# The late modulation's rows loaded in quarters on GpSimd's own queue, into a buffer of their own, begun while RWKV is prepared

## The chip, the cores and the metric

The kernel runs on one core of a Trainium2 chip. The metric is the time of one execution on the device in microseconds (us): a median over runs, and beside it one execution taken by the hardware profiler, from which all rows below are read. In the profile PE is TensorE (PEld its weight loads), DVE is VectorE, ACT is ScalarE, POOL is GpSimd, SP is SyncE, which here only issues DMAs. "SPq" and "POOLq" are the queues in which an engine's DMAs wait in order.

## What is computed

The reference runs two transformer blocks, one after the other, over 512 tokens of width 1024 in float32. Only the first has the part that is changed: all its norms are modulated by a vector that comes from a condition `c`.

```python
mod = jax.nn.silu(c) @ ada_w[l] + ada_b[l]
sh_m, sc_m, g_m, sh_f, sc_f, g_f = jnp.split(mod[:, None, :], 6, axis=-1)

h = rmsnorm(x, norm_g[l, 0]) * (1.0 + sc_m) + sh_m
p = h @ w_in[l]
p_a, p_b, p_c = split_cols(p, (N_RWKV_IN, N_FOX_IN, N_NSA_IN))
y_a = rwkv7_mix(p_a, ...)
y_b = fox_mix(p_b, ...)
y_c = nsa_mix(p_c, ...)
y = jnp.concatenate([y_a, y_b, y_c], axis=-1) @ w_out[l]
x = x + g_m * rmsnorm(y, norm_g[l, 1])
h = rmsnorm(x, norm_g[l, 2]) * (1.0 + sc_f) + sh_f
f = conv_ffn(h, ...)
x = x + g_f * rmsnorm(f, norm_g[l, 3])
```

`sh_m` and `sc_m` are needed at the start. The other four sections of `mod`, here called the late modulation, are needed only after `w_out`. `ada_w` is 1024 x 6144, 24 MB, of which 16 MB are late. In `rwkv7_mix` the key is normalised head by head (`kk / max(norm(kk), 1e-12)`), and the head's output `y` is normalised by its mean and variance after the recurrence.

## The kernel before

**Stages.** From the start to about 60 us the first modulation and the RWKV projection run. Then come `prep(0)` and `prep(1)`, which make the operands of the RWKV recurrence for two halves of its channels, then `core(0)` and `core(1)` in turns, which run the recurrence in chunks of 64 tokens. Beside the cores run `side` (`compress`, `fox`, `stacks`: the compressed keys, the FoX attention, keys laid out for the NSA attention). All of these generators leave gaps on PE, and `fill(n)` puts matmuls of the projections (`proj_t`, `proj_n`) into them, one or two after each of their steps. After the cores come the NSA attention, `project_out` and the rest of the kernel.

**What sets the order.** A scheduler orders the instructions of each engine by the order in which the code emits them and by its own estimate of when each is ready. Each engine then runs its list strictly in order and waits where an operand or a free buffer is missing. A DMA belongs to the list of the engine that issues it. Nearly all loads are on SP's.

**Streamed weights.** `Weights.load` (L263) loads the next block of weights, 128 partitions x up to 1024, on SP's queue (L269) into the tile `raw`, which has three buffers. `Weights.next` then has ScalarE write the rounded high part `whi` (L278) and VectorE the rest `wlo` (L279), three buffers each. Projections use both.

**The late modulation.** `some_ada` (L623) treats one of 16 matrices (sections 1 and 2, eight row blocks `k`), 128 x 2048 each. It takes two `raw` buffers in turn, loads 512 KB into each on SP's queue (L631), and GpSimd multiplies each of the eight 128 x 256 pieces by a column of `sil` (L635 the first, L637 the others) and adds them up in `am` (L638), four buffers. A call later (`owing`) PE sums `am` over the partitions with `ones` and VectorE adds the bias into `mod`. `some_ada` is called on every second turn of the core loop (AE = 2, L956), and the rest after it (`some_ada(99)`).

**Head norms.** `head_rsq` (L721) runs in each `prep` (on `kk`) and at the end of each `core` (on `y`). PE sums squares by head (`psr<-x,sq`), VectorE writes `hv` (L298 is its helper's line), GpSimd raises it to -0.5 as `hr` (L733), VectorE spreads it as `nr` (L735), and PE transposes that back (L738). GpSimd also turns the loaded masks into 8 bit as `im` (L688). In `compress`, `kk` (L1020, L1021) and the weights `w` (L1029) come on SP's queue, VectorE adds a position term into `kr`, PE multiplies by `w` into `psa`, and VectorE and ScalarE form `ch` for a second matmul.

Of the kernel before, what the change touches and what calls it, by code (L numbers as in the profile page):

```python
# [10 lines left out]
F32 = mybir.dt.float32  # L11
# [7 lines left out]
P = 128  # L19
# [236 lines left out]
class Weights:  # L256


    def __init__(self, nc, pool, src, raw_bufs, bufs):
        self.nc, self.pool, self.src, self.raw_bufs, self.bufs = nc, pool, src, raw_bufs, bufs  # L260
        self.i = 0

    def load(self, label):  # L263
        nc, i = self.nc, self.i
        lab, bl = PLAN[i]
        assert lab == label, (lab, label)
        n = sum(len(c) for _, _, c in bl)
        raw = self.pool.tile([P, 1024], F32, name="raw", bufs=self.raw_bufs)
        nc.sync.dma_start(raw[:, :n], self.src[i][:, :n])  # L269
        self.i += 1  # L270
        return raw[:, :n]
# [12 lines left out]
def two_blocks(ctx, tc, ins, out):  # L284
    nc = tc.nc
    S, V, G, PE = nc.scalar, nc.vector, nc.gpsimd, nc.tensor
# [18 lines left out]
    MUL, ADD, SUB, MAX, MIN = ALU.mult, ALU.add, ALU.subtract, ALU.max, ALU.min  # L305

    const = ctx.enter_context(tc.tile_pool(name="const", bufs=1))
    wpool = ctx.enter_context(tc.tile_pool(name="wts", bufs=1))
    upool = ctx.enter_context(tc.tile_pool(name="u", bufs=1))
    dram = ctx.enter_context(tc.tile_pool(name="dram", bufs=1, space=bass.MemoryType.DRAM))  # L310
    W = Weights(nc, wpool, ins["wst"], 3, 3)
# [22 lines left out]
    sil = const.tile([P, 8], F32, name="sil")  # L334
# [283 lines left out]

    owing = []

    def some_ada(n=1):

        for _ in range(n):  # L623
            if not todo and not owing:
                return
            if todo:
                sec, k = todo.pop(0)
                am = st.tile([P, 256], F32, name="am", bufs=4)
                for q in range(2):
                    aw = wpool.tile([P, 4, 256], F32, name="raw", bufs=W.raw_bufs)  # L630
                    nc.sync.dma_start(aw.rearrange("p a b -> p (a b)"), ins["ada"][sec, k][:, q * 1024:(q + 1) * 1024])  # L631
                    for r in range(4):
                        s = sil[:, 4 * q + r:4 * q + r + 1]
                        if q + r == 0:
                            G.tensor_scalar(am, aw[:, r], s, 1.0, op0=MUL, op1=MUL)  # L635
                            continue
                        G.tensor_scalar(aw[:, r], aw[:, r], s, 1.0, op0=MUL, op1=MUL)  # L637
                        G.tensor_tensor(am, am, aw[:, r], op=ADD)  # L638
                owing.append((sec, k, am))
            if len(owing) > 1 or not todo:  # L640
                sec, k, am = owing.pop(0)
                ps = bank(f"r{k % 2}", 2)
                for s in range(2):
                    mm(ps[:, s:s + 1], am[:, s * P:(s + 1) * P], ones[:, 0:1])
                j = 16 * sec + k
                tt(mod[:, j:j + 9:8], ps[:, :2], vc("ada_b", j, 9)[:, ::8], ADD)
# [303 lines left out]
        return lambda ps: act(dst, ps, AF.Copy, scale=scale)  # L950

    LO = 0
    FP, FN, NS, FC, NA, OR, AE = 1.6,2.4,3,(2.2,2.6),5,0,2
    jobs = [proj_t("nsa", copy_to(kcv[0])), proj_t("nsa", copy_to(kcv[1])), proj_n("nsa_n", 280, 2, evac_n),
            proj_n("fox_n", 384, 2, lambda b, ps: act(fv[:, b], ps, AF.Copy))]
    for j in range(3):  # L956
# [15 lines left out]
    def fill(n):  # L972
        with later():
            owed[0] += n
            while owed[0] >= 1:
                owed[0] -= 1
                next(work[0], None)
# [182 lines left out]

    kst = []
    prep, core, spare = rwkv(phA.enter_context(tc.tile_pool(name="rp", bufs=1, reuse_waits="tile")))
    for t in range(2):
        for _ in prep(t):
            fill(FP)
    for _ in work[0]:
        pass
    pA.close()
# [22 lines left out]
    for _ in work[0]:  # L1191
        pass
    some_ada(99)
    phA.close()
    nm[0] = 2
    psm = blk.enter_context(tc.tile_pool(name="psb", bufs=1, space=PSUM, reuse_waits="tile"))
# [345 lines left out]
    q = SqSum(fp)  # L1542
# [538 lines left out]
```

## Time and profile before

| | us |
|---|---|
| median of 3 runs | 2184.73 |
| lowest and highest | 2183.6, 2187.89 |
| the profiled execution | 2183.81 |
| its span in the trace | 2182.0 |

The late modulation and the stages around it lie in the first sixth of the span. A row of a timeline gives the start, the duration, the engine, the line, the operation, what it writes and reads with their shapes, and in square brackets how long the engine had been idle before it and on what. A row of a window gives the busy time of each engine within it; PEclk is the TensorE clock that was granted, as a share of 2.4 GHz, so 0.50 is the level of 1.2 GHz.

### The profile page before, as it was taken

The page shows a single profiled execution, that of the slowest core. Times are in us where ns is not written, and L with a number is a line of the kernel's source. Part 1 is how long each engine was busy: PE and PEld are TensorE (multiplying, and loading weights), DVE is VectorE, ACT ScalarE, POOL GpSimd, SP SyncE. Part 2 cuts the span into 40 slices and gives each one's busy share as a digit, 9 for nine tenths or more (in the row PEclk, how much of TensorE's full clock was granted, in tenths as well). Part 3 has the DMA queues.
Part 4 walks back from the last instruction along what each step waited for, and adds up shares of the span by engine and source line. Part 5 has one row for each costly group of instructions (what it writes and reads, how often), then busy time and mean ns, then how long its engine had stood idle before and what let it go on. Part 6 is the DMA issues. An engine that isn't in the chain of part 4 may idle for free.

```text
span 2182.0 us, 31649 instructions
## 1 busy us (share of the span) xinstructions
PE 2134.6 (98%) x12498; PEld 1762.1 (81%) x12498; DVE 1142.8 (52%) x2171; ACT 785.9 (36%) x1332; POOL 496.4 (23%) x538
## 2 busy tenths in 40 slices
PE   7989999999999999899999999999999999999999
PEld 5878777667888888788888899998877888888887
DVE  6553445666752664653344449957554455433442
ACT  4422223553542442332222335445453233222221
POOL 3168662232000000320011024333221022100110
PEclk9989998998999999999999999999999999999999
DMA  8344335102532222222222343342352222222222
GB/s 309 102 145 157 109 137 145 40 21 88 165 133 97 98 97 87 70 96 98 97 98 98 126 152 107 100 128 76 111 145 86 95 92 96 97 97 97 98 97 85
DMA packets 84846, 238.31 MB, mean 109 GB/s; under 512 B 13970, under 2 KB 21448, under 8 KB 84570
## 3 DMA queue, kind: packets, MB, share of 16 engines
q1 hardware_dynamic: 78874, 226.19, 30.9%
q0 software_dynamic: 5104, 9.52, 1.2%
q8 instruction: 98, 1.61, 0.3%
q10 hardware_dynamic: 720, 0.57, 0.1%
q14 instruction: 50, 0.41, 0.1%
HBM read 216.02 MB, written 15.33 MB: 106 GB/s over the span
## 4 chain that ended last, share of the span: by engine, by line
PE 75%; DVE 1%; ACT 1%; issue 0%; POOL 0%; ACTq 0%; DVEq 0%; POOLq 0%
PE mm L288 68%; PE pS L288 3%; PE pO L288 2%; PE pT L1666 1%; PE pT L1649 1%; PE pT L288 0%; PE pst L288 0%; DVE xa L303 0%; PE psm L288 0%; DVE wlo L279 0%; DVE tmp L1487 0%; PE pso L288 0%; DVE ul L303 0%; PE lps L288 0%; ACT whi L278 0%
## 5 line engine op out<-in xcount | busy, mean ns | idle before, releaser
L278 ACT ACTIVATE whi<-raw 128x1024 fp32r<-128x1024 f32 (+4 forms) x312 | 325.7, 1046 | 836.0 <-PE mm L288 619.8
L279 DVE TENSOR_TENSOR wlo<-raw,whi 128x1024 fp32r<-128x1024 f32 (+4 forms) x303 | 373.9, 1235 | 343.3 <-ACT whi L278 339.6
L288 PE MATMUL mm<-ul,whi 128*128 128x512 f32 (+1 forms) x1280 | 494.9, 388 | 1.8 <-DVE ul L303 1.8
L288 PE MATMUL mm<-uh,wlo 128*128 128x512 f32 (+1 forms) x1280 | 494.4, 387 | 0.5 <-DVE wlo L279 0.5
L288 PE MATMUL mm<-uh,whi 128*128 128x512 f32 (+1 forms) x1280 | 489.7, 388 | 2.1 <-ACT uh L291 1.2
L288 PEld LDWEIGHTS mm<-ul,whi 128*128 128x128 f32 x1280 | 241.7, 189 | 52.5 <-DVE ul L303 2.8
L288 PEld LDWEIGHTS mm<-uh,whi 128*128 128x128 f32 x1280 | 239.9, 189 | 52.3 <-ACT uh L291 1.8
L288 PEld LDWEIGHTS mm<-uh,wlo 128*128 128x128 f32 x1280 | 241.8, 189 | 48.8 <-DVE wlo L279 0.9
L288 PE MATMUL mm<-hh,wlo 128*128 128x512 f32 (+1 forms) x550 | 209.3, 381 | 0.0
L288 PE MATMUL mm<-hl,whi 128*128 128x512 f32 (+1 forms) x550 | 209.3, 381 | 0.0
L288 PE MATMUL mm<-hh,whi 128*128 128x512 f32 (+1 forms) x550 | 208.4, 381 | 0.0
L1516 POOL TENSOR_TENSOR gg<-gg,R 128x512 f32<-128x512 f32 x44 | 77.4, 1762 | 473.4 <-ACT gg L291 473.4
L288 PE MATMUL mm<-whi,uh 128*128 128x256 f32 (+1 forms) x488 | 140.5, 288 | 0.0
L288 PE MATMUL mm<-whi,ul 128*128 128x256 f32 (+1 forms) x488 | 139.8, 287 | 0.0
L288 PE MATMUL mm<-wlo,uh 128*128 128x256 f32 (+1 forms) x488 | 139.2, 285 | 0.0
L288 PEld LDWEIGHTS mm<-hl,whi 128*128 128x128 f32 x550 | 103.4, 188 | 19.8
L288 PEld LDWEIGHTS mm<-hh,whi 128*128 128x128 f32 x550 | 103.4, 188 | 19.7
L288 PEld LDWEIGHTS mm<-hh,wlo 128*128 128x128 f32 x550 | 103.4, 188 | 19.6
L291 ACT ACTIVATE p<-p,smin 128x128 f32<-128x128 f32 (+4 forms) x136 | 81.8, 602 | 92.8 <-DVE smin L1077 52.6
L294 DVE TENSOR_TENSOR gh<-mm,gg 128x512 f32<-128x512 f32 x44 | 30.4, 691 | 131.1 <-PE mm L288 125.5
L288 PEld LDWEIGHTS mm<-whi,ul 128*128 128x128 f32 x488 | 93.1, 191 | 1.7 <-issue 1.5
L288 PEld LDWEIGHTS mm<-whi,uh 128*128 128x128 f32 x488 | 93.0, 191 | 1.4 <-issue 0.4
(532 smaller groups left out, 3433.8 us busy)
## 6 DMA issues: line engine op xcount, KB each, us to landing
raw<-in_wst_dram SPq DMA_DIRECT2D x294, 512.0 KB, 3.2
raw<-in_ada_dram SPq DMA_DIRECT2D x32, 512.0 KB, 4.7
aw<-in_ada_dram SPq DMA_DIRECT2D x16, 512.0 KB, 8.4
raw<-in_wst_dram SPq DMA_DIRECT2D x8, 448.0 KB, 6.0
ka<-d POOLq DMA_DIRECT2D x1, 3570.0 KB, 49.5
k<-d POOLq DMA_DIRECT2D x1, 2556.0 KB, 17.1
part<-in_x_dram SPq DMA_DIRECT2D x4, 512.0 KB
xa<-in_x_dram SPq DMA_DIRECT2D x8, 256.0 KB, 3.6
```

The costliest lines, as they stand in the source:

```text
L278: nc.scalar.activation(hi[:, :n], w, AF.Copy)
L279: (e or nc.vector).tensor_tensor(lo[:, :n], w, hi[:, :n].bitcast(F32), op=ALU.subtract)
L288: PE.matmul(o, l, r, start=start, stop=stop)
L291: S.activation(o, i, f, **kw)
L294: V.tensor_tensor(o, a, b, op=op)
L1516: G.tensor_tensor(g, g, R, op=MUL)
L1649: PE.transpose(ps[:, (j * nb + b) * P:(j * nb + b + 1) * P], xn[:, (b * n + j) * P:(b * n + j + 1) * P], ident)
L1666: PE.transpose(ps[:, j:j + P], p[:, o + j:o + j + P], ident)
```

## The change

The late matrices no longer use `raw` and SP's queue. They come as 64 quarters of 256 KB, issued by GpSimd, into the two halves of one tile `raws`, and the load of the next quarter is issued ahead of the work on the present one. `raws` is taken from the streamed weights: `raw` keeps two buffers, and a weight goes to the third, now `raws`, only while `W.spare` is true, which it isn't from before `prep` until after `some_ada(99)`. `some_ada` is called on every tenth step of both `prep`, four times in all, and on every third turn of the core loop instead of every second.

```diff
--- before.py
+++ after.py
@@ -258,14 +258,17 @@
 
     def __init__(self, nc, pool, src, raw_bufs, bufs):
         self.nc, self.pool, self.src, self.raw_bufs, self.bufs = nc, pool, src, raw_bufs, bufs
-        self.i = 0
+        self.i = self.n = 0
+        self.spare = True
 
     def load(self, label):
         nc, i = self.nc, self.i
         lab, bl = PLAN[i]
         assert lab == label, (lab, label)
         n = sum(len(c) for _, _, c in bl)
-        raw = self.pool.tile([P, 1024], F32, name="raw", bufs=self.raw_bufs)
+        last = self.spare and self.n % self.raw_bufs == self.raw_bufs - 1
+        self.n += 1
+        raw = self.pool.tile([P, 1024], F32, name="raws" if last else "raw", bufs=1 if last else self.raw_bufs - 1)
         nc.sync.dma_start(raw[:, :n], self.src[i][:, :n])
         self.i += 1
         return raw[:, :n]
@@ -618,24 +621,44 @@
 
     owing = []
 
+    def pieces():
+
+        ax = wpool.tile([P, 4, 256], F32, name="raws", bufs=1)
+        order = [(sec, k, q) for sec in (1, 2) for k in range(8) for q in range(4)]
+
+        def load(i):
+            sec, k, q = order[i]
+            h = ax[:, 2 * (i % 2):2 * (i % 2) + 2]
+            G.dma_start(h.rearrange("p a b -> p (a b)"), ins["ada"][sec, k][:, q * 512:(q + 1) * 512])
+            return h
+
+        h = load(0)
+        for i in range(len(order)):
+            nxt = load(i + 1) if i + 1 < len(order) else None
+            yield h
+            h = nxt
+
+    rows = pieces()
+
     def some_ada(n=1):
 
         for _ in range(n):
             if not todo and not owing:
                 return
             if todo:
-                sec, k = todo.pop(0)
-                am = st.tile([P, 256], F32, name="am", bufs=4)
-                for q in range(2):
-                    aw = wpool.tile([P, 4, 256], F32, name="raw", bufs=W.raw_bufs)
-                    nc.sync.dma_start(aw.rearrange("p a b -> p (a b)"), ins["ada"][sec, k][:, q * 1024:(q + 1) * 1024])
-                    for r in range(4):
-                        s = sil[:, 4 * q + r:4 * q + r + 1]
+                am = None
+                for q in range(4):
+                    h = next(rows)
+                    if q == 0:
+                        sec, k = todo.pop(0)
+                        am = st.tile([P, 256], F32, name="am", bufs=4)
+                    for r in range(2):
+                        s = sil[:, 2 * q + r:2 * q + r + 1]
                         if q + r == 0:
-                            G.tensor_scalar(am, aw[:, r], s, 1.0, op0=MUL, op1=MUL)
+                            G.tensor_scalar(am, h[:, 0], s, 1.0, op0=MUL, op1=MUL)
                             continue
-                        G.tensor_scalar(aw[:, r], aw[:, r], s, 1.0, op0=MUL, op1=MUL)
-                        G.tensor_tensor(am, am, aw[:, r], op=ADD)
+                        G.tensor_scalar(h[:, r], h[:, r], s, 1.0, op0=MUL, op1=MUL)
+                        G.tensor_tensor(am, am, h[:, r], op=ADD)
                 owing.append((sec, k, am))
             if len(owing) > 1 or not todo:
                 sec, k, am = owing.pop(0)
@@ -950,7 +973,7 @@
         return lambda ps: act(dst, ps, AF.Copy, scale=scale)
 
     LO = 0
-    FP, FN, NS, FC, NA, OR, AE = 1.6,2.4,3,(2.2,2.6),5,0,2
+    FP, FN, NS, FC, NA, OR, AE = 1.6,2.4,3,(2.2,2.6),5,0,3
     jobs = [proj_t("nsa", copy_to(kcv[0])), proj_t("nsa", copy_to(kcv[1])), proj_n("nsa_n", 280, 2, evac_n),
             proj_n("fox_n", 384, 2, lambda b, ps: act(fv[:, b], ps, AF.Copy))]
     for j in range(3):
@@ -1160,9 +1183,12 @@
 
     kst = []
     prep, core, spare = rwkv(phA.enter_context(tc.tile_pool(name="rp", bufs=1, reuse_waits="tile")))
+    W.spare = False
     for t in range(2):
-        for _ in prep(t):
+        for i, _ in enumerate(prep(t)):
             fill(FP)
+            if i % 10 == 9:
+                some_ada()
     for _ in work[0]:
         pass
     pA.close()
@@ -1191,6 +1217,7 @@
     for _ in work[0]:
         pass
     some_ada(99)
+    W.spare = True
     phA.close()
     nm[0] = 2
     psm = blk.enter_context(tc.tile_pool(name="psb", bufs=1, space=PSUM, reuse_waits="tile"))
```

Lines of the changed kernel are shifted: L733 is L756 there, L635, L637 and L638 are L658, L660 and L661, L269 is L272, L278 is L281.

On GpSimd, before, from the end of the first modulation (`am` from `aw`) on. Both `hr` here are those of `prep`:

```order
L573 TENSOR_TENSOR am_562<-am_562,aw 128x256 x3
L577 TENSOR_TENSOR am<-am,am_562 128x256
L688 CAST im<-imf 128x320 x2
L733 TENSOR_TENSOR hr<-hv,mhalf 128x8 x2
L635 TENSOR_SCALAR am<-raw,sil 128x256
L637 TENSOR_SCALAR raw<-raw,sil 128x256 x3
L638 TENSOR_TENSOR am<-am,raw 128x256
L637 TENSOR_SCALAR raw<-raw,sil 128x256 x2
L638 TENSOR_TENSOR am<-am,raw 128x256
```

GpSimd, changed, the last rows ahead of the first `hr` (`am` and `raws` belong to the late matrices):

```order
L660 TENSOR_SCALAR raws<-raws,sil 128x256
L661 TENSOR_TENSOR am<-am,raws 128x256 x2
L658 TENSOR_SCALAR am<-raws,sil 128x256
L660 TENSOR_SCALAR raws<-raws,sil 128x256
L632 DMA raws<-in_ada_dram 128x512
L661 TENSOR_TENSOR am<-am,raws 128x256
L632 DMA raws<-in_ada_dram 128x512
L660 TENSOR_SCALAR raws<-raws,sil 128x256 x2
L661 TENSOR_TENSOR am<-am,raws 128x256
L756 TENSOR_TENSOR hr<-hv,mhalf 128x8
L660 TENSOR_SCALAR raws<-raws,sil 128x256 x2
```

Ahead of the first `hr` there are now 20 scalings (TENSOR_SCALAR), 16 additions (TENSOR_TENSOR on `raws`), the two casts and 9 loads, all behind the first modulation's last addition but for two further loads that stand before it. Between the first and the second `hr` stand 14 scalings, 13 additions and 7 loads. The cores' two `hr` were behind all late matrices before and are so now.

On SP's queue, before, from the last weights loaded during `prep` on:

```order
L269 DMA raw<-in_wst_dram 128x1024 x2
L631 DMA raw<-in_ada_dram 128x1024
L993 DMA cf<-in_cmat_dram 128x128
L631 DMA raw<-in_ada_dram 128x1024
L269 DMA raw<-in_wst_dram 128x1024
L631 DMA raw<-in_ada_dram 128x1024 x3
L1020 DMA kk_1255<-kcv_109 64x512
L1021 DMA kk_1255<-kcv_109 64x511
L1009 DMA dcum<-cum 6x512
L1020 DMA kk_1260<-kcv_109 64x512
L1021 DMA kk_1260<-kcv_109 64x511
L1029 DMA w_1266<-in_ck_dram 128x512
```

SP's queue, changed, at the same place:

```order
L272 DMA raw<-in_wst_dram 128x1024 x2
L1016 DMA cf<-in_cmat_dram 128x128
L272 DMA raw<-in_wst_dram 128x1024 x4
L1043 DMA kk_1349<-kcv_109 64x512
L1044 DMA kk_1349<-kcv_109 64x511
L1032 DMA dcum<-cum 6x512
L1153 DMA fb<-dcum 128x512
L1043 DMA kk_1354<-kcv_109 64x512
L1044 DMA kk_1354<-kcv_109 64x511
L1052 DMA w_1360<-in_ck_dram 128x512
```

The five late loads there (L631, now none) are gone from among the mask `cf` and the loads of `kk` and `w`.

On ScalarE, at the end of the cores, changed (`y<-psr` are the copies of the two cores' output, `whi<-raws` the first weight of `project_out`; before, the three `whi` stood further ahead, among the queries `nq` of the last projections):

```order
L294 ACTIVATE y<-psr_3509 128x512
L281 ACTIVATE whi<-raws 128x1024
L281 ACTIVATE whi<-raw 128x1024 x2
L294 ACTIVATE p,ssum<-p,smin 128x512
L294 ACTIVATE y<-psr_3558 128x512
L294 ACTIVATE sq<-y 128x512 x2
```

Before, the same three `whi` on ScalarE:

```order
L291 ACTIVATE nq_96<-psm 128x512
L278 ACTIVATE whi<-raw 128x1024
L291 ACTIVATE p,ssum<-p,smin 128x256
L291 ACTIVATE nq_97<-psm 128x512
L278 ACTIVATE whi<-raw 128x1024
L291 ACTIVATE uh<-fq_103 128x512
L291 ACTIVATE uh<-fq_104 128x512
L278 ACTIVATE whi<-raw 128x1024
```

They now stand between the two copies of `y`.

## Rows read from the trace of the kernel before

**Rows 1.** Page, first section: busy time of each engine, share of span, instructions.

```profile
PE 2134.6 (98%) x12498; PEld 1762.1 (81%) x12498; DVE 1142.8 (52%) x2171; ACT 785.9 (36%) x1332; POOL 496.4 (23%) x538
```

**Rows 2.** Windows: us, busy of PE, PEld, DVE, ACT, POOL, PEclk, DMA share, GB/s.

```profile
111.30:118.30 7.00, 2.69 (x16) 1.88 (x15) 3.00 (x6) 0.00 (x0) 1.64 (x1) 0.82 0.00 0
118.30:122.70 4.40, 4.40 (x14) 3.88 (x13) 3.29 (x6) 1.05 (x2) 0.00 (x0) 0.51 0.00 0
146.50:150.00 3.50, 1.60 (x13) 1.49 (x13) 2.84 (x5) 0.00 (x0) 3.50 (x5) 0.99 0.59 192
150.00:163.60 13.60, 12.73 (x116) 10.94 (x116) 4.92 (x8) 2.04 (x3) 10.57 (x17) 0.50 0.76 245
175.70:179.70 4.00, 0.12 (x4) 0.00 (x0) 3.50 (x9) 1.23 (x3) 4.00 (x7) 1.00 0.49 112
180.70:190.90 10.20, 10.20 (x84) 9.10 (x81) 1.39 (x2) 2.62 (x4) 7.55 (x13) 0.50 0.67 234
365.00:490.00 125.00, 122.40 (x772) 87.51 (x772) 79.47 (x305) 66.60 (x202) 37.12 (x55) 1.00 0.18 54
```

**Rows 3.** Timeline, GpSimd: start, us, operation, [idle before <- what ended it].

```profile
59.05 0.72 POOL L577 TENSOR_TENSOR am<-am,am 128x256 f32<-128x256 f32 x1
...
86.28 1.67 POOL L733 TENSOR_TENSOR hr<-hv,mhalf 128x8 f32<-128x8 f32 x1 [20.11 <-DVE hv L298]
112.57 1.64 POOL L733 TENSOR_TENSOR hr<-hv,mhalf 128x8 f32<-128x8 f32 x1 [24.62 <-DVE hv L298]
...
346.82 1.65 POOL L733 TENSOR_TENSOR hr<-hv,mhalf 128x8 f32<-128x8 f32 x1 [22.94 <-DVE hv L298]
```

**Rows 4.** Groups, GpSimd, 120 to 370 us: busy us, mean ns of one | idle before.

```profile
L638 POOL TENSOR_TENSOR am<-am,raw 128x256 f32<-128x256 f32 x112 | 86.4, 780 | 4.7
L637 POOL TENSOR_SCALAR raw<-raw,sil 128x256 f32<-128x256 f32 x112 | 57.5, 530 | 27.1 <-DMA raw<-in_ada_dram 26.7 <-DMA raw<-in_wst_dram 0.3
```

**Rows 5.** Lines 468, 499, issued by GpSimd: ns min/median/max, first and last start.

```profile
L468 POOL DMA_DIRECT2D l<-in_lines_dram x1: 567/567/567, 2.0 to 2.0; - x1
...
L499 POOL DMA_DIRECT2D ka<-d x3: 1084/1091/1217, 517.1 to 575.2; - x3
```

**Rows 6.** DMA issues: count, KB each, median us from issue to landing.

```profile
raw<-in_ada_dram SPq DMA_DIRECT2D x32, 512.0 KB, 4.7
...
w<-in_ck_dram SPq DMA_DIRECT2D x4, 256.0 KB, 3.0
...
l<-in_lines_dram POOLq DMA_DIRECT2D x1, 210.4 KB, 7.0
```

**Rows 7.** Timeline, VectorE, behind the first prep step's power.

```profile
87.98 0.43 DVE L735 COPY nr<-hr 128x512 f32<-128x512 f32 x1 [1.78 <-POOL hr L733]
...
89.99 0.74 DVE L279 TENSOR_TENSOR wlo<-raw,whi 128x560 fp32r<-128x560 f32 x1 [0.40 <-ACT whi L278]
```

**Rows 8.** Timeline, PE, at the transposes of both prep steps.

```profile
91.16 0.60 PE L738 MATMUL psr<-cm,nr 128*128 128x128 f32 x4
...
114.72 0.66 PE L738 MATMUL psr<-cm,nr 128*128 128x128 f32 x4 [2.44 <-DVE nr L735]
117.25 2.05 PE L288 MATMUL psr<-rk,x 128*128 128x512 f32 x2 [1.88 <-DVE rk L303]
```

**Rows 9.** Waits of SP's queue, 60 to 400 us: total us, times, longest.

```profile
SPq L631 <- POOL am L638: 79.3, 20, 8.7
```

**Rows 10.** Timeline, PE, at the compression's matmuls.

```profile
147.83 1.07 PE L288 MATMUL psa<-kr,w 128*128 128x62 f32 x8 [1.34 <-DMA w<-in_ck_dram]
149.48 1.56 PE L288 MATMUL psa<-kr,w 128*128 128x62 f32 x8 [0.57 <-DMA w<-in_ck_dram]
...
179.72 0.31 PE L288 MATMUL psa<-ch,w 128*64 128x31 f32 x4 [3.89 <-DVE ch L294]
```

**Rows 11.** Timeline, VectorE, at the compression's sums.

```profile
175.37 1.14 DVE L294 TENSOR_TENSOR kr<-kk,vec 128x248 f32<-128x248 f32 x2 [7.05 <-DMA kk<-kcv]
```

**Rows 12.** Timeline, ScalarE, the second copy of y.

```profile
341.28 0.60 ACT L291 ACTIVATE y<-psr 128x512 f32<-128x512 f32 x1 [0.85 <-PE psr L288]
```

## Prediction

> **What bounds the kernel now.** I read the page's first section first: TensorE (PE) is busy for 98% of the span [rows 1], so a change can only give back PE's idle time or its time at the lower clock, or add to them. The chain of waits runs back only into block 1's attention stage and never reaches the stretch that is changed, so that stretch (59 to 365 us) is read by stage, from windows and timelines. From 365 us on PE is busy, 122.4 of the next 125 us [rows 2], so a delay of the core's end goes on to the end of the program one for one. In the windows the reader is to see two things. PE waits: 2.69 us busy in the 7.0 us from 111.3, 1.60 in 3.5 from 146.5, 0.12 in 4.0 from 175.7. And behind each wait stands a stretch with PE full at a granted clock of 0.50 or 0.51, the 1.2 GHz level: 4.4, 13.6 and 10.2 us [rows 2]. Then GpSimd's timeline: idle from 59.8 us up to the first prep step's power `hr` at 86.28, but for the two casts, idle again until the second at 112.57, and idle 22.94 us before the core's at 346.82 [rows 3]. That idle time is what the change fills.
>
> **What moves.** The 16 late matrices keep their arithmetic: 8 scalings and 7 additions each, 8 x 0.53 + 7 x 0.78 = 9.7 us of GpSimd a matrix [rows 4]. Their 32 loads of 512 KB leave SP's queue and become 64 of 256 KB on GpSimd's. By the excerpts the first `hr` stands behind 20 scalings, 16 additions, the two casts and 9 load issues; between the two `hr` stand 14, 13 and 7; the core's two stand behind all the rest.
>
> **Price of a load on GpSimd.** An issue keeps the engine for 0.57 us in the one load from HBM, and 1.08 to 1.22 in the larger moves [rows 5]; I take 0.57, since that load's size (210 KB) is nearest. The landing is not shown for this form. The nearest rows: 256 KB on SP's queue lands in 3.0 us, 512 KB of these matrices in 4.7, the GpSimd load in 7.0, at the program's start [rows 6]. I take 4.0: the nearest row by size and source is SP's, and the one GpSimd row pulls it up. The next load is issued ahead of a quarter's 2 + 2 operations (2 x 0.53 + 2 x 0.78 = 2.6 us), so each awaited load costs 4.0 - 2.6 = 1.4 us (0.4 at 3.0, 2.1 at 4.7, 4.4 at 7.0).
> The Trainium skill speaks for cheaper: "DMA: Bandwidth & Descriptors", section "Anatomy of one DMA — SWDGE (gpsimd) path", fits about 2 us and 436 KB a us, which makes an estimate of 2.6 us for 256 KB. No row here shows such a load, and the one from HBM that does exist took 7.0 [rows 6]. By that fit no landing wait would be left, and the sum would be rival A's below.
>
> **First `hr`.** GpSimd is free at 59.8. Work: 20 x 0.53 + 16 x 0.78 + 1.3 (casts) = 24.4 us. Issues: 9 x 0.57 = 5.1. That alone gives 89.3. Landings: 8 x 1.4 = 11.2, so 100.5 instead of 86.28 [rows 3, 4]. What covers it is projection work: PE came to the transposes that need it at 91.2 [rows 8]; `nr` was ready (87.98 + 0.43) 2.1 us after `hr` began [rows 7]. With two more matmuls ahead now, `hr` may begin as late as 89.3 at no cost. So the stall is 100.5 - 89.3 = 11.2 us. Behind the copy `nr` on VectorE stands a weight's low half, `wlo`, that the projection needs next: 0.40 + 0.74 = 1.2 more [rows 7]. After the stall PE runs at the lower clock: 2.2 us lost in the 4.4 us after 118.3, some 6.4 in the 13.6 us after 150 [rows 2]; I take 3.5. Together 16 us (0 with no landing waits, 6 at 0.4 a load, 24 at 2.1).
>
> **Second `hr`.** PE's own shift of 16 puts its input at 112.6 + 16 = 128.6. GpSimd gets there at 100.5 + 1.7 + 14 x 0.53 + 13 x 0.78 + 7 x (0.57 + 1.4) = 133.5. PE already waits there, 2.44 us for `nr` and 1.88 for `rk` [rows 8], so nothing covers it: +5. Prep: **+21 us**.
>
> **The core's gain.** SP's queue runs in order, and the late loads on it wait for a free buffer, 79.3 us in 20 waits on GpSimd's additions between 60 and 400 us [rows 9]; all behind them wait too. Without them the compression's loads come early: PE's waits of 1.34 and 0.57 us on `w` and of 3.89 on `ch` go [rows 10], the last since VectorE had sat 7.05 us before `kr` for the load of `kk` [rows 11], and `ch` is computed behind it. That is 5.8 us. With these waits the slow stretches behind them may go: 12.7 us busy at 0.50 and 10.2 at 0.50 are worth 6.4 and 5.1 us [rows 2]. Other short waits stay near by, so I take 60%, 7 us. **-13 us** (-6 to -17). Next late there are the projection's own weights on ScalarE, which I cost at nothing: the queue that brings them is empty of late rows now.
>
> **The core's end.** Unhindered, GpSimd's 16 matrices take 16 x (9.7 + 4 x 1.97) = 281 us, and with casts and `hr` they end at 59.8 + 281 + 4.6 = 346, near the 346.82 of the core's `hr` [rows 3]; PE's shift of some +7 by then covers it. But the third weight buffer is the late rows' until they end, so project_out's first weight lands some 3 us after, and by the excerpt its three ScalarE casts now stand ahead of the second `y` copy, at 341.28 before [rows 12], on which the core's `hr` hangs. +3 us (0 to 8; if landings are 4.7 us the matrices end near 391 and this term is +44).
>
> **Sum.** 21 - 13 + 3 = +11 us on the profiled execution's 2183.8 (its span is 2182.0; it lies 0.9 below the median of 2184.7): **2195 us**.
>
> **Rivals.** *A, faster: the loads are free.* If a load costs 0.57 and lands within 2.6 to 3 us, GpSimd reaches `hr` at 89.3 to 92, prep stalls by 0 to 3, matrices end by 330, and the core's gain of 13 stays, less 0 to 3 at its end: **2172**. For it: the equal loads on SP's queue, 3.0 [rows 6]. Against it: 7.0 in the only GpSimd row of this kind; and there is no slack, since the bare work already ends at 89.3. It decides below some 0.4 us of wait a load.
> *B, no change.* Landing waits of about 0.8 us: `hr` at 96, prep +12, core -13, end +2: **2185**.
> *C, slower by far: GpSimd becomes the bound of the whole stage.* Landing as in the 7.0 us row: 16 x (9.7 + 4 x 4.97) + 64 = 538 us for the matrices' end against 346.82, so the core's `hr` and all behind it wait: **about 2375**; from a landing of 4.6 us on this, and no longer the stall in prep, sets the time (4.7: about 2228). For it: that row. Against it: it was issued at 2.0 us, beside the start's other loads. The Trainium skill names a way to it: "SBUF — State Buffer", section "SBUF: two separate sides", says that while VectorE runs two-port operations GpSimd can't write the descriptors of its own loads. No load of the trace of before was issued by GpSimd beside steady VectorE work, so the traces neither bear it out nor exclude it.
> *D, the change doesn't do what it says* has no case: the excerpts show the loads on GpSimd's queue ahead of `hr`.
>
> **How the numbers follow.** Forecast (a stall in prep that outweighs the core's gain, +5 to +30): 0.46. A 0.28, B 0.17, C 0.09. Faster by over 0.2% (4.4 us, about what a measurement of this kernel can tell from no change) is A and B's lower edge, 0.29; within 0.2%, most of B, 0.16; slower 0.55. The range leaves out A's lower quarter and most of C: 2168 to 2222. Cases of both signs hold much of the chance; the forecast's own range is 2189 to 2214.
>
> **What would show it.** The first `hr` at about 100 us with GpSimd busy or waiting on `raws` just before, a PE wait of about 11 us on `nr`, then a stretch at 0.50; the second near 133. Median landing of the 64 loads 4.0. PE's waits on `w` and `ch` gone; SP without its waits on the additions; the matrices' end near 346. Wrong if `hr` begins before 90 (then A), if the landing wait is hidden, or if the slow stretches of the core stay (then the sum is +18).

## The result, and the profile after

| | us |
|---|---|
| before, median (4 runs) | 2186.25 |
| changed, median (4 runs: 2202.1 to 2206.06) | 2204.09 |
| ratio, 95% interval | 1.009 [1.0077, 1.0104] |
| span of the profiled execution, before and changed | 2182.0, 2203.7 |

The change costs 17 to 23 us. The forecast was +11 us: its direction was right, but its size was little more than half of what came. The first section of the page now reads as follows (busy time, share of the span, instructions); it answers to [rows 1].

```profile
PE 2140.1 (97%) x12498; PEld 1764.4 (80%) x12498; DVE 1151.3 (52%) x2171; ACT 787.6 (36%) x1332; POOL 544.0 (25%) x602
```

PE does the same 12498 matmuls. Its busy time grew by 5.5 us and the span by 21.7, so most of the loss is waiting. GpSimd's timeline at the first power `hr` (L756 now) and just before the second, to be set against [rows 3]: start, duration, operation, idle before it and what ended that.

```profile
91.98 0.59 POOL L632 DMA_DIRECT2D raws<-in_ada_dram  x1
92.59 0.74 POOL L661 TENSOR_TENSOR am<-am,raws 128x256 f32<-128x256 f32 x1
93.63 0.56 POOL L632 DMA_DIRECT2D raws<-in_ada_dram  x1 [0.30 <-POOL am L661]
94.97 0.93 POOL L660 TENSOR_SCALAR raws<-raws,sil 128x256 f32<-128x256 f32 x2 [0.78 <-DMA raws<-in_ada_dram]
95.87 0.71 POOL L661 TENSOR_TENSOR am<-am,raws 128x256 f32<-128x256 f32 x1
96.55 1.67 POOL L756 TENSOR_TENSOR hr<-hv,mhalf 128x8 f32<-128x8 f32 x1
...
128.22 0.73 POOL L661 TENSOR_TENSOR am<-am,raws 128x256 f32<-128x256 f32 x1
128.90 1.67 POOL L756 TENSOR_TENSOR hr<-hv,mhalf 128x8 f32<-128x8 f32 x1
```

Both `hr` follow a late addition with no gap: they waited for the engine, not for their input. PE's timeline at the places of [rows 8] and [rows 10]:

```profile
99.04 1.12 PE L761 MATMUL psr<-cm,nr 128*128 128x128 f32 x4 [6.81 <-DVE nr L758]
...
131.09 1.12 PE L761 MATMUL psr<-cm,nr 128*128 128x128 f32 x4 [8.50 <-DVE nr L758]
134.18 2.04 PE L291 MATMUL psr<-rk,x 128*128 128x512 f32 x2 [1.98 <-DVE rk L306]
...
170.95 2.37 PE L291 MATMUL psa<-kr,w 128*128 128x62 f32 x10 [8.87 <-DMA w<-in_ck_dram]
...
201.12 0.31 PE L291 MATMUL psa<-ch,w 128*64 128x31 f32 x4 [1.56 <-DVE ch L297]
```

Two stalls of 6.81 and 8.50 us on `nr` in `prep`, where there was one of 2.44; and in the core a wait of 8.87 us on the compression's weight `w`, where there were 1.34 and 0.57. The windows behind these stalls (us, busy of PE, PEld, DVE, ACT, POOL, granted clock, DMA share, GB/s), for [rows 2]:

```profile
122.00:140.00 18.00, 7.38 (x25) 5.80 (x25) 7.27 (x13) 0.10 (x1) 16.32 (x24) 0.64 0.19 70
...
161.50:171.00 9.50, 0.63 (x13) 0.42 (x9) 4.66 (x8) 0.00 (x0) 4.35 (x8) 0.67 0.59 190
171.00:180.00 9.00, 9.00 (x47) 7.67 (x49) 0.85 (x2) 0.00 (x0) 7.94 (x14) 0.59 0.39 124
201.00:214.00 13.00, 12.88 (x148) 11.28 (x148) 1.77 (x3) 3.70 (x6) 8.51 (x13) 0.61 0.51 172
```

Behind each of them stands a stretch near the 1.2 GHz level, whole or in part (0.59 from 171 to 180 us, 0.61 from 201 to 214). So the core kept its slow stretches.

For the profiled executions (2183.81 and 2205.47 us) a ledger comes from the starts of the same operation in both traces. Second transposes: 131.09 against 114.72, +16.4. First `w` matmul: 170.95 against 147.83, +23.1. `ch` matmul: 201.12 against 179.72, +21.4. Second copy of `y`: 360.85 against 341.28, +19.6. First `hr` of the cores: 366.10 against 346.82, +19.3. The span: +21.7. The loss is made in `prep` (16.4) and at the core's start (6.7 more); of the latter the core gives 3.5 back by the second copy of `y`.

GpSimd's groups of the late work from 58 to 360 us (busy us, mean ns of one, idle before them and on what), which answer to [rows 4]:

```profile
L661 POOL TENSOR_TENSOR am<-am,raws 128x256 f32<-128x256 f32 x112 | 89.5, 800 | 4.7
L660 POOL TENSOR_SCALAR raws<-raws,sil 128x256 f32<-128x256 f32 x112 | 65.1, 588 | 52.6 <-DMA raws<-in_ada_dram 51.9
L632 POOL DMA_DIRECT2D raws<-in_ada_dram x62 | 36.2, 584 | 7.7 <-POOL am L661 7.7
L658 POOL TENSOR_SCALAR am<-raws,sil 128x256 f32<-128x256 f32 x16 | 11.2, 699 | 23.8 <-PE psr L291 18.7 <-DMA raws<-in_ada_dram 5.0
```

The page's part on DMA issues has this row for the late loads (count, KB each, median us to landing):

```profile
raws<-in_ada_dram POOLq DMA_DIRECT2D x64, 256.0 KB, 2.9
```

It answers to [rows 6]. The late rows now run on GpSimd from 60.29 us to 353.0, 293 us; before they ran from 127.64 to 323.9, 196 us. The arithmetic grew by 13 us (152.9 before, by the same groups). New are 36 us of issuing and 8 us of waiting for the engine's own addition before an issue; the waits for landings are 57 us (45 before) and those for PE to free a sum 19 (7 before). So the work begins 67 us earlier and ends 29 us later.

### The profile page after: what moved, and what is told of

Its sections match the earlier page's. It is cut to its first block, busy times and chain, and to the rows that moved or that the text cites. A ratio compares the mean times of both kernels' runs of the same rounds, so it can differ in the third digit from the quotient of the medians.

```text
span 2203.7 us, 31654 instructions
## 1 busy us (share of the span) xinstructions
PE 2140.1 (97%) x12498; PEld 1764.4 (80%) x12498; DVE 1151.3 (52%) x2171; ACT 787.6 (36%) x1332; POOL 544.0 (25%) x602
## 4 chain that ended last, share of the span: by engine, by line
PE 89%; DVE 4%; DMA 3%; POOL 2%; ACT 1%; issue 1%; SPq 0%; DVEq 0%; ACTq 0%; POOLq 0%
PE mm L291 67%; PE psm L291 4%; PE psr L291 4%; PE pS L291 3%; PE pss L291 2%; PE pO L291 2%; PE pso L291 2%; DMA raws<-in_ada_dram 1%; PE pT L1693 1%; PE psa L291 1%; PE pst L1124 1%; PE k L291 1%; POOL raws L660 1%; PE pT L1676 1%; DVE wlo L282 1%
## 5 line engine op out<-in xcount | busy, mean ns | idle before, releaser
L281 ACT ACTIVATE whi<-raw 128x1024 fp32r<-128x1024 f32 (+4 forms) x216 | 224.8, 1042 | 560.4 <-PE mm L291 428.0
L282 DVE TENSOR_TENSOR wlo<-raw,whi 128x1024 fp32r<-128x1024 f32 (+4 forms) x210 | 262.5, 1250 | 237.2 <-ACT whi L281 233.2
L281 ACT ACTIVATE whi<-raws 128x1024 fp32r<-128x1024 f32 (+2 forms) x96 | 101.3, 1055 | 250.6 <-PE mm L291 204.4
L282 DVE TENSOR_TENSOR wlo<-raws,whi 128x1024 fp32r<-128x1024 f32 (+1 forms) x93 | 115.0, 1237 | 91.3 <-ACT whi L281 91.1
L291 PEld LDWEIGHTS mm<-hl,whi 128*128 128x128 f32 x550 | 103.4, 188 | 19.6
```

Source lines behind the costliest of these rows:

```text
L281: nc.scalar.activation(hi[:, :n], w, AF.Copy)
L282: (e or nc.vector).tensor_tensor(lo[:, :n], w, hi[:, :n].bitcast(F32), op=ALU.subtract)
L291: PE.matmul(o, l, r, start=start, stop=stop)
```

## Experiments

All comparisons are with the kernel before. The table gives the time and then where the loss stands: starts in us of the second transposes (PE), the `ch` matmul (PE), the last matmul `psr<-NF,MT` of the recurrence (PE), the second copy of `y` (ScalarE), and the last late additions (GpSimd). The starts are of one profiled execution of each kernel, which lies up to 7 us from that kernel's median (e9 the furthest, then e2, e13 and e5), so differences of a few us between rows are to be read with that in mind.

| kernel | ratio, 95% interval | second transposes | `ch` | last `NF,MT` | second `y` | last late addition |
|---|---|---|---|---|---|---|
| before | | 114.7 | 179.7 | 329.8 | 341.3 | 322.3 |
| changed | 1.009 [1.0077, 1.0104] | 131.1 | 201.1 | 349.4 | 360.8 | 352.3 |
| e1_noprep | 1.0086 [1.0072, 1.0100] | 129.8 | 185.9 | 335.1 | 364.0 | 356.0 |
| e2_sparelate | 1.0163 [1.0146, 1.0179] | 115.0 | 172.8 | 336.7 | 348.2 | 368.8 |
| e3_hrfirst | 1.0164 [1.0149, 1.0180] | 117.0 | 187.1 | 372.1 | 382.6 | 348.0 |
| e4_split_sp | 1.0049 [1.0033, 1.0066] | 128.1 | 191.8 | 339.3 | 351.6 | 334.0 |
| e5_hr_off | 1.0028 [1.0017, 1.0039] | 124.0 | 194.4 | 342.5 | 354.0 | 345.4 |
| e6_spare_end | 1.0055 [1.0043, 1.0067] | 130.3 | 185.9 | 333.5 | 352.8 | 360.0 |
| e7_before_actq | 1.0005 [0.9994, 1.0015] | 115.8 | 181.2 | 335.8 | 347.3 | 328.4 |
| e8_both_off | 0.9991 [0.9980, 1.0003] | 116.8 | 179.3 | 318.9 | 335.8 | 349.6 |
| e9_gated | 1.0064 [1.0050, 1.0078] | 117.1 | 183.5 | 340.9 | 361.4 | 341.1 |
| e10_hr_off_nocalls | 1.0054 [1.0039, 1.0068] | 115.0 | 174.7 | 325.8 | 351.3 | 343.5 |
| e11_after_end | 1.0072 [1.0059, 1.0086] | 132.9 | 201.7 | 350.0 | 358.0 | 352.8 |
| e12_gated3 | 1.0083 [1.0067, 1.0099] | 116.8 | 182.4 | 325.8 | 360.2 | 341.2 |
| e13_after_actq | 1.0094 [1.0079, 1.0109] | 129.8 | 199.7 | 346.4 | 357.9 | 349.3 |
| e14_gated3_never | 1.0011 [1.0000, 1.0023] | 114.6 | 180.0 | 326.3 | 350.7 | 345.4 |

The theory: `hr` behind late rows makes the loss, and the core's gain fails for a reason of its own. The rivals: the calls in `prep`, the quarters' issue on GpSimd, or the missing third buffer make the loss.

**What puts late rows ahead of `hr`.**

e1_noprep, and e4_split_sp, which has the last edit below as well:

```diff
-        for i, _ in enumerate(prep(t)):
+        for _ in prep(t):
             fill(FP)
-            if i % 10 == 9:
-                some_ada()
...
-    FP, FN, NS, FC, NA, OR, AE = 1.6,2.4,3,(2.2,2.6),5,0,3
+    FP, FN, NS, FC, NA, OR, AE = 1.6,2.4,3,(2.2,2.6),5,0,2
...
-            G.dma_start(h.rearrange("p a b -> p (a b)"), ...)
+            nc.sync.dma_start(h.rearrange("p a b -> p (a b)"), ...)
```

> The changed kernel without the four calls in prep, and with AE back at 2. In the scheduled order GpSimd still has 16 additions and 9 awaited loads ahead of the first hr, because the late rows' own buffer is free from the start. Theory (hr stands behind late rows, whatever the calls are): the prep stall stays, first hr near 96 us, 2200 to 2208 us. Rival (the calls in prep are the cause): the stall goes, 2184 to 2188 us, or 2172 if the core then gains its 13 us.

> As e1 but the 64 quarters are issued on SP's queue instead of GpSimd's: the buffer of their own and the quarters alone. GpSimd has 22 additions ahead of the first hr, and weights on SP's queue stand behind late quarters. Theory (the own buffer, which lets late work go ahead of hr, is what costs): slower than the kernel before by 15 to 45 us, 2200 to 2230. Rival (issue from GpSimd, its 0.6 us each and the landings, is what costs): within 5 us of the kernel before, 2180 to 2190.

e1: `hr` at 97.2 and 127.6 us, the stall stays: 1.0086. The calls are not needed for it. With a buffer of its own, free from the start, late work is scheduled ahead of `prep` wherever in the code it is called. e4: the first `hr` stands at 99.9 and PE waits 9.70 us on `nr`, so the first stall stays with SP's queue too. The second `hr` (125.9) waits for its input there and not for the engine, and PE's wait on it is 2.45 us, as in the kernel before. The time is 2193.9 us, 1.0049, below the theory's 2200 and above the rival's 2190. Its last late addition starts at 334.0 instead of 356.0. So the own buffer makes the stall, and issuing on GpSimd costs another 8.6 us between e1 (2202.56) and e4, which goes with the second stall and the longer chain of late work; how it divides between them was not tried.

**`hr` taken off GpSimd.** e5_hr_off edits the changed kernel:

```diff
-            G.tensor_tensor(r, v, mhalf, op=ALU.pow)
+            if op == MAX:
+                ts(r, v, 0.0, 0.0, MUL, ADD)
+            else:
+                G.tensor_tensor(r, v, mhalf, op=ALU.pow)
```

> The changed kernel, but in prep hr is no longer made on GpSimd: VectorE writes zeros in its place in one short operation. This leaves out the power, so the normalised key is zero; all other work stays. Theory (the prep loss is hr waiting in GpSimd's order behind late rows): no PE wait on nr above 1 us, second transposes 1 to 3 us earlier than in the kernel before instead of 16 later, and 2178 to 2190 us in all, the lower half if the core then also gains. Rival (two weight buffers or the additional DMA traffic slow prep by themselves): 2196 us or more, with PE waits on wlo instead of nr.

2192.25 us, 1.0028: 12 us of the 18 are gone with the stall. What is left in `prep` has another cause, not one of the two expected. PE's timeline of e5:

```profile
107.85 1.01 PE L291 MATMUL psr<-ones,am 128*128 128x1 f32 x4 [5.17 <-POOL am L661]
...
124.04 0.66 PE L764 MATMUL psr<-cm,nr 128*128 128x128 f32 x4 [0.72 <-DVE nr L761]
```

PE waits 5.17 us for a late sum that the calls in `prep` have put into its own order; behind the stall on `hr` of the changed kernel that sum is ready in time. e10 leaves the calls out as well (with AE at 2, as in e1), and e8 also returns the third buffer later:

```diff
     some_ada(99)
-    W.spare = True
...
     for _ in work[0]:
         pass
+    W.spare = True
     sq = SqSum()
```

> e5 without the four calls in prep and with AE 2 (hr of prep replaced by zeros written on VectorE, which leaves out the power), third buffer back where the change puts it. Against e5 it shows what the calls cost, against e8 what the return of the third buffer costs. Theory: PE's wait of 5.2 us on the late sums in prep goes, but ScalarE waits at the core's end for project_out's first weight as in e1: 2186 to 2196 us, at the core's start 8 to 12 us ahead of e5. Rival (the calls cost nothing by themselves): shift at the core's start as in e5.

> e6 and e5 together: no calls in prep, third buffer back only after project_out, and hr of prep replaced by zeros written on VectorE (leaves out the power). Both suspected costs are gone, late rows still run through prep on GpSimd's own queue. Theory: the core's gain is all that is left, 2170 to 2178 us. Rival (quarters on GpSimd's queue with the third buffer reserved cost something else): 2182 us or more.

e10's second transposes begin at 115.0, as in the kernel before (114.7): `prep` then loses nothing, which shows that neither the loads nor the two weight buffers slow it by themselves, and that the calls cost e5 its 9 us there. And the core gains: `ch` comes 5.0 us early in e10, the last `NF,MT` 4.0 (e10) and 10.9 (e8). But the time is 1.0054 and 0.9991. The gain is lost at the core's end. In e10 PE waits 13.7 us on the second `y`, in e1 9.9. ScalarE's timeline of e1 there:

```profile
350.19 0.19 ACT L294 ACTIVATION_READ_ACCUMULATOR p<-p,smin 128x1 f32 x1
360.16 1.06 ACT L281 ACTIVATE whi<-raws 128x1024 fp32r<-128x1024 f32 x1 [9.79 <-DMA raws<-in_wst_dram]
361.12 1.99 ACT L281 ACTIVATE whi<-raw 128x1024 fp32r<-128x1024 f32 x2
363.01 0.58 ACT L294 ACTIVATE y<-psr 128x512 f32<-128x512 f32 x1
```

ScalarE holds `y` for 9.79 us because a cast stands ahead of it whose weight waits for the third buffer until the last late row has left it (356.7 us). In e8 that wait is gone, and another one shows. GpSimd's timeline of e8:

```profile
347.92 0.93 POOL L660 TENSOR_SCALAR raws<-raws,sil 128x256 f32<-128x256 f32 x2 [0.74 <-DMA raws<-in_ada_dram]
348.82 1.51 POOL L661 TENSOR_TENSOR am<-am,raws 128x256 f32<-128x256 f32 x2
350.29 1.67 POOL L759 TENSOR_TENSOR hr<-hv,mhalf 128x8 f32<-128x8 f32 x1
```

PE's timeline of e8 just after it:

```profile
352.48 1.11 PE L764 MATMUL psr<-cm,nr 128*128 128x128 f32 x4 [7.51 <-DVE nr L761]
```

The core's own `hr` stands behind the last late rows, and PE waits 7.51 us for it.

**The core's end alone.** e6_spare_end is e1, e11_after_end the changed kernel, both with the edit on `W.spare` above.

> As e1 (no calls in prep, AE 2), and the weights get the third buffer back only after project_out instead of before it, so that project_out's first weight doesn't wait for the last late row. Theory (e1 loses some 14 us at the core's end because ScalarE stands with that weight's cast ahead of the copy of y): the wait of 9.9 us of PE on y goes, prep still loses 15, 2188 to 2194 us. Rival (the last late rows themselves end too late, the cores' hr stand behind them): 2199 to 2204 us.

> The changed kernel with one edit: the weights get the third buffer back only after project_out. Theory (in the changed kernel the late rows end early enough by the shift of 20 us, so that the copy of y waits for nothing): 2200 to 2208 us, no change. Rival (it is paid at the end here too): 2188 to 2197 us.

e6: 2197.63, 5 us below e1 and 4 us above what was expected: the wait on `y` goes (352.8 instead of 364.0), but PE waits on `nr` once more at the cores' end (6.6 us, beside 15.3 in `prep`). e11: 2199.33, just under the theory's 2200, with an interval that overlaps the changed kernel's, so between nothing and some 5 us is paid at this place in the changed kernel.

**The order rebuilt with all work kept.** In e2_sparelate (e1, with the buffer given up only when the cores begin) late work can't start in `prep`. In e3_hrfirst and e9_gated the late scalings read a copy of the scale that GpSimd makes behind `hr`:

```diff
-    W.spare = False
     for t in range(2):
...
+    W.spare = False
     decays(spare)
```
```diff
             G.tensor_tensor(r, v, mhalf, op=ALU.pow)
+            if op == MAX:
+                G.tensor_scalar(z, r, 0.0, 1.0, op0=MUL, op1=MUL)
+                G.tensor_tensor(gate[0], z, sil, op=ADD)
...
-                        s = sil[:, 2 * q + r:2 * q + r + 1]
+                        s = gate[0][:, 2 * q + r:2 * q + r + 1]
```

> As e1, but the weights keep the third buffer until the cores begin, so no late row can start before that and both prep hr come ahead of all late work on GpSimd; loads still in quarters on GpSimd's queue. Theory (all of the loss is the prep stall, and the core gains nothing because the streamed weights, with two buffers, hold SP's queue instead of the late rows): no PE wait on nr beyond the 2.4 us of before, 2184 to 2190 us. Rival (the core's gain of 13 us exists and was only hidden by the late start): 2170 to 2176 us.

> The changed kernel with a data dependency that lets late work of prep begin only behind that prep's hr: each hr is followed by two tiny operations on GpSimd that copy the condition's scale behind hr, and the late scalings read the copy. One late matrix is called in prep(0), two in prep(1), AE 2. The weights have two buffers from prep on. Theory: first hr back at 86 us, stall in prep under 3 us, 2184 to 2190 us, as e2 within 4 us. Rival (the two weight buffers or the loads slow prep by themselves): over 2194 us. Rival (core gain): 2172 to 2178 us.

Both expectations failed: `prep` is free of the stall (second transposes 115.0 and 117.0), and both are 35 us slower than before. In e2 the core runs up to 7 us ahead (`ch` 172.8), but late rows end at 369.5, and ScalarE's timeline shows what that does:

```profile
348.18 0.60 ACT L294 ACTIVATE y<-psr 128x512 f32<-128x512 f32 x1 [0.98 <-PE psr L291]
372.89 1.06 ACT L281 ACTIVATE whi<-raws 128x1024 fp32r<-128x1024 f32 x1 [24.11 <-DMA raws<-in_wst_dram]
```

ScalarE stands 24.11 us for the third buffer, and PE 24.6 behind it. In e3 PE waits 18.4 us on late sums and 11.6 on `nq`. So in the changed kernel the stall in `prep` buys an earlier end of the late rows; in these two, without that start, the same price is paid, and more, on late sums or at the core's end.

e9 also starts one matrix ahead of `prep`, returns the buffer late and has PE sum two calls later, not one; e12 three calls later; e14 is e12 without the return of the buffer. The edits of e14 (e9 has 2 in place of the 3):

```diff
-            if len(owing) > 1 or not todo:
+            if len(owing) > 3 or not todo:
...
     some_ada(99)
-    W.spare = True
```

> The changed kernel rearranged so that no hr of prep stands behind late rows: one matrix starts ahead of prep, one may start behind the first hr, the others behind the second (a copy of the condition's scale made on GpSimd behind each hr is what the late scalings read); AE 2, matrices summed by PE two calls late instead of one, third buffer back only after project_out. All work is done. Theory (GpSimd's order is what costs; the core's gain of e8 is 6 to 15 us until its end): first hr within 3 us of 86, no PE wait on nr above 3 us in prep, matrices done by 330, 2170 to 2180 us. Rival (PE then waits for the late sums, as in e3, or the core's end gives the gain back): 2184 to 2195 us.

> e9 with the matrices summed by PE three calls late instead of two; else the same, all work done. Theory (e9 lost its gain to PE's waits of 17 us in all on late sums that GpSimd had not finished): these fall under 6 us, 2178 to 2189 us. Rival (the late start of most matrices behind the second hr costs by itself): 2193 us or more, the shift at the cores' end as in e9.

> e12, but the weights never get the third buffer back. In e12 (and e6, e8, e9, e11, which give it back behind project_out) the schedule still put the first load into that buffer ahead of project_out's own loads on SP's queue, where it waited for the last late row (e12: until 341.96 us, PE waiting 11 us behind it). Theory (that wait is what took e12's gain at the cores' end): the cores end 0 to 6 us ahead of the kernel before instead of 19 behind, 2176 to 2186 us. Rival (two weight buffers for the rest of the program cost as much, or another wait at the cores' end takes the place): 2192 us or more.

e9: PE's waits on late sums are still 17.0 us in five, 1.0064. e12: 1.8 us of them, and the last `NF,MT` comes 4.0 us ahead of the kernel before; then 11 us are lost at once. SP's queue in e12's timeline:

```profile
341.96 0.33 SPq L272 DMA_DIRECT2D raws<-in_wst_dram  x1
342.38 9.05 SPq L272 DMA_DIRECT2D raw<-in_wst_dram  x3
```

ScalarE's timeline of e12 beside it:

```profile
348.76 1.06 ACT L281 ACTIVATE whi<-raw 128x1024 fp32r<-128x1024 f32 x1 [13.93 <-DMA raw<-in_wst_dram]
349.73 0.58 ACT L294 ACTIVATE nq<-psm 128x512 f32<-128x512 f32 x1
```

The load into the third buffer stands ahead of the loads of the next weights and waits for the last late row. e14 takes it away: 1.0011 [1.0000, 1.0023], no difference that could be measured, or a loss below 0.25%. Its stall in `prep` is that of the kernel before, by PE's timeline:

```profile
114.64 0.66 PE L767 MATMUL psr<-cm,nr 128*128 128x128 f32 x4 [2.47 <-DVE nr L764]
```

It is 3.5 us ahead at the last `NF,MT` and 9.4 behind at the second `y`, after a wait of 4.78 us on a late sum at 331.34. That is the best order with all work kept that was found for late rows on GpSimd's own queue, and it does not beat the kernel before.

**What holds `w`.** e7_before_actq is the kernel before and e13_after_actq the changed one, both with this edit on the three loads of `compress`:

```diff
-                nc.sync.dma_start(kk[0:64], ...)
+                S.dma_start(kk[0:64], ...)
...
-                nc.sync.dma_start(w1, ...)
+                S.dma_start(w1, ...)
```

> The kernel before, with one edit: the compression's loads of kk and w are issued by ScalarE instead of SP, so they no longer stand behind late rows in SP's queue. No late row moves. Theory (the core's gain exists: PE's waits on w and ch and the stretch at the lower clock behind the first): 2172 to 2179 us. Rival (the gain was a misreading; something else is late next, or ScalarE is held up by waiting for the buffers): 2182 to 2190 us.

> The changed kernel with one edit: the compression's loads of kk and w are issued by ScalarE instead of SP. Theory (PE's wait of 8.9 us on w comes from SP's queue, where those loads stand behind streamed weights that wait for wlo with two buffers): w is issued some 6 us sooner, the wait falls under 3 us, and 2194 to 2200 us in all. Rival (w comes late for another reason, as in e7, where ScalarE issued it no sooner): the wait stays at 6 us or more, 2201 to 2206 us.

Both theories fell. e7: 1.0005; PE still waits 1.60 us on `w`, then 4.4 on `kct` and 3.0 on `X`. ScalarE issues `w` no sooner there (146.4 us, SP before 144.74), so e7 does not show what an earlier `w` would be worth. e13: ScalarE issues `w` at 162.5 instead of 164.95 on SP, PE waits 6.7 us instead of 8.87, and the time is that of the changed kernel, 1.0094. SP's place in the queue is worth 2 us there and not 9. Some 3 us more are the landing: 6.1 us in the changed kernel and 5.6 in e13 against 3.0 [rows 6]. What sets the rest was not settled.

Two comparisons between the runs go further. SP's queue before, then in e10, where `prep` runs as before and no late row is on it, each with a row of SP's waits there:

```profile
141.10 0.43 SPq L1009 DMA_DIRECT2D dcum<-cum  x1
144.74 1.75 SPq L1029 DMA_DIRECT2D w<-in_ck_dram  x2
...
SPq L1029 <- DMA dcum<-cum: 1.8, 1, 1.8
```
```profile
145.09 0.30 SPq L1035 DMA_DIRECT2D dcum<-cum  x1
146.64 1.06 SPq L1055 DMA_DIRECT2D w<-in_ck_dram  x2
...
SPq L1035 <- DVE cum L1034: 4.1, 1, 4.1
```

So `w` came no earlier when the late rows had left SP's queue. Before, it waited 1.8 us for the DMA that moves `cum` out, and that one was issued 0.1 us after VectorE had finished `cum` (139.53 + 1.43 us); in e10 SP stands 4.1 us for `cum` (4.0 in the changed kernel). It hung on that chain in all three, not on late rows. All the same, the slow stretch behind `w` can go. PE at `w` in e1, and its windows from there on, to be set against [rows 2] and [rows 10]:

```profile
161.56 1.97 PE L291 MATMUL psa<-kr,w 128*128 128x62 f32 x16 [0.26 <-DMA w<-in_ck_dram]
```
```profile
161.50:171.00 9.50, 9.44 (x164) 8.55 (x166) 4.70 (x7) 2.14 (x3) 4.64 (x6) 1.00 0.49 160
171.00:183.00 12.00, 11.14 (x184) 9.60 (x178) 7.78 (x14) 3.08 (x4) 10.61 (x15) 1.00 0.40 131
```

The clock stays at 1.00 where it was 0.50 before, and e1's shift falls from +15.3 us at `psr<-rk,x` (132.53 against 117.25) to +6.2 at `ch`. The kernels divide by the calls in `prep`. In those without them (e1, e2, e4, e6, e8, e10) PE waits at most 1.4 us on `w` (in e4 it waits 4.7 on another operand there). With them it waits 8.9 (changed), 7.0 (e5), 9.0 (e11), 6.7 (e13), 5.3 (e12) and 5.9 (e14), but not in e3 and e9, where it has waited some 10 us on late sums instead. AE is 2 in e12 and e14 too, so it is not that. How the calls bring the wait about was not tried: in the changed kernel `w` is issued 7.2 us later than in e1 (164.95 against 157.78), while PE reaches it at about the same time (162.1 and 161.3).

## Why the prediction was right or wrong, point by point

- **Price of a load.** The issue was right (584 ns, taken as 570). The landing was 2.9 us and not 4.0, nearest to SP's row of 3.0 [rows 6] that the text named the nearest and then left. The Trainium skill's "DMA: Bandwidth & Descriptors", section "Anatomy of one DMA — SWDGE (gpsimd) path", gave an estimate of 2.6 us; by that rule the trace agrees within 0.3. What was drawn from it, no landing wait and rival A, did not hold: the next issue waited 0.30 us for the engine's own addition in 26 cases and some issues stood late among the arithmetic, so that 47 of the 64 quarters waited, 1.2 us in the mean.
- **First `hr`.** Forecast 100.5, measured 96.55; stall 11.2, measured 6.81. Mechanism right, size off mainly by the landing: the waits for quarters ahead of it add up to some 3.5 us, not 11.2. e1 and e4 (own buffer) and e10 (stall gone, transposes at 115.0) show it.
- **Second `hr`.** Forecast 133.5, +5 us; measured 128.90, and 8.50 - 2.44 = +6.1.
- **Prep as a whole.** Forecast 16 for the first stall with what follows it, and 5 for the second, +21; measured +10.3 when PE comes to the second transposes (122.59 against 112.28) and +6.1 there, +16.9 at `psr<-rk,x` (134.18 against 117.25). Nearly right, and what is missing is the smaller first stall. The lower clock behind the second (0.64 from 122 to 140 us) is not in these numbers, and what it costs was not separated.
- **The core's gain: the step that failed.** The forecast took -13 us from "the compression's loads come early". The waits of SP's queue on late additions did go, as it said. But `w` came later, not earlier: 8.87 us of waiting. PE's wait on `ch` fell from 3.89 to 1.56, but the slow stretches stayed, so from `psr<-rk,x` to the second `y` the shift went from +16.9 to +19.6. The text gives +18 for the case that the slow stretches stay, and +17.8 came by the medians; that is partly luck, since its +18 still counts 5.8 us of waits as gone. The error was to read `w` as late because it stands behind late rows: before as in e10, which has no late rows on that queue and issues it no earlier (146.64 against 144.74), it hung on `cum`, which VectorE makes. And the forecast took the gain in full for a change that also puts calls into `prep`: with them PE waits longer on `w`, without them (e1) 9.1 us come back between `psr<-rk,x` and `ch`. SP's waits also only changed their name: L272 waits 158.4 us on `wlo` now from 60 to 420 us (L269 before: 36.0, from 60 to 400), with two buffers for weights. The row of SP's waits in the changed kernel (total us, times, longest):

```profile
SPq L272 <- DVE wlo L282: 158.4, 21, 28.5
```

- **A gain there exists, but is not kept.** e8, e10, e12 and e14 run 3.5 to 11 us ahead of the kernel before at the last `NF,MT`, and e1 and e6 have won back 10 and 12 us since `psr<-rk,x` by then. The forecast priced the core's end at +3, without asking what the gain would meet there: the last late addition of e8, e10, e12 and e14 starts at 341 to 350 us, that of e1 and e6 at 356 and 360, and the core's `hr`, `y` or the next weights wait for it. "Next late there ... I cost at nothing" was the sentence that should have been worked out.
- **The matrices' end.** Forecast 346, measured 353.0; right in kind. In the changed kernel itself the cores come 20 us later too, so that little is paid (e11: 0 to 5 us).
- **Rivals.** A needed `hr` before 90. B's `hr` at 96 came (96.55), but not its time: `prep` lost 16.9 and not 12, and the core gave nothing. C's long landing did not come (2.8 to 6.2 us). The point of the Trainium skill's "SBUF — State Buffer", section "SBUF: two separate sides", that VectorE's two-port operations hold up such loads, is not borne out here: 64 loads beside a VectorE that was busy half the time landed in 2.9 us. How many of VectorE's operations are of the two-port kind the trace does not tell.

## What to carry to other kernels

Work put on an idle engine that runs in order stands ahead of the short operations that others wait for. Add up the bare work that gets ahead of them, with issues and landings, against the time at which they are needed; and expect that a buffer that is free early pulls such work forward wherever the code calls it.

A wait seen in a queue is a gain only if nothing else is late at the same place: ask what else the load waits for, and look at a kernel in which it alone has moved. Price every part of a change by itself; here the calls in `prep` took back what the moved loads gave. And a chain that starts earlier must also end earlier to help; here it started 67 us earlier, took 97 us longer, and ended 29 later.

## What was not expected of the hardware

GpSimd waits 0.30 us after its own addition before it issues a load into that buffer, 26 times. Landings of its 256 KB loads were steady: 2.8 at the least, 2.9 in the middle, 6.2 at the most. Its scalings took 588 ns in the mean (530 before) and single pairs up to 3.3 us, beside a busy VectorE; that the two are linked was not tried.
